# A hybrid RWKV-7 and MoBA layer on one Trainium2 core: the two heads of a pair take turns on the halves of TensorE's array

## The chip, the core and the metric

The kernel runs on one core of a Trainium2 chip. The core has a matrix engine (TensorE, PE in the profile), a vector engine (VectorE, DVE), an engine for functions of one variable (ScalarE, ACT), a general engine (GpSimd, POOL), SyncE (SP), which issues most transfers here, and 16 DMA engines. They work side by side, each takes its own instructions in their order, and semaphores make one wait for another. Matmuls write to PSUM, from which VectorE and ScalarE read; everything else lies in SBUF. Both have 128 partitions. The metric is device time in microseconds (us): 842.22 before, the median of 3 runs (840.99 to 842.25).

## What is computed

One decoder layer for 256 tokens of width 2048, in float32. One projection of the normalised input feeds two branches, whose results are gated, added and projected back:

```
h = rms_norm(x);  p = h @ w_in                         # 2048 x 12416
y_a = rwkv7_mix(p_r, p_k, p_v, p_wd, p_ad) * silu(z_a)  # 16 heads of 64
y_b = moba_attention(p_q, p_kq, p_vq) * silu(z_b)       # 16 heads of 64
merged = sigmoid(g_a) * (y_a @ w_proj_rwkv) + sigmoid(g_b) * (y_b @ w_proj_moba)
out = x + merged @ w_out
```

For 256 tokens the block-sparse attention has a single block, so it is causal attention with normalised queries and keys: softmax(q k / 8, masked) v for each head. The RWKV recurrence is computed in 4 chunks of 64 tokens: within a chunk the products of keys with keys and of keys with queries are needed, masked, and from these a triangular system is solved.

## The kernel before

**The dense work.** The weights stream through SBUF in loads of 1 MB. Each load makes two jobs. A job's half of the weights is split by ScalarE (`hi`, L216) and VectorE (`lo`, L222) into two parts, and TensorE multiplies in three passes, hi by hi, lo by hi and hi by lo: 24 matmuls of 128x256 (L329) where the result is wanted feature by feature, 12 of 128x512 (L347 to L349) where it is wanted token by token. Splits run two jobs ahead.

**The side work.** Everything else (RWKV, attention, norms) is written as generators (`rwkv_elem`, `rwkv_r`, `inverse`, `rwkv_v`, `moba`, ...). They stand in one queue, and after each job the next piece of the first of them, up to its `yield`, is written behind the job. Urgent ones (`trans` in `qk_post`, `group_norm`) advance after every job as well. The heads come in two groups of eight (g = 0, 1), and each piece of side work is done once for each group. The order that counts on the engines is not quite that of the code: a scheduler of the framework places instructions by its own estimates, and may put dense matmuls between those of a piece.

**Heads and halves.** Two heads of 64 features share 128 partitions: head p = 0 of a pair lies in partitions 0 to 63, p = 1 in 64 to 127; fi = 0 to 3 counts the pairs of a group. A matmul on one head's keys thus uses 64 rows of the array, and one that writes one head's values uses 64 columns. In the profile such shapes stand as rows*columns: 64*128, 128*64, 64*64; the dense matmuls are 128*128. A matmul on float32 leaves two records of PE in the trace, one on float32r (the dense ones) and a transpose one.

**What the change touches.** In `rwkv_r`, for each pair and head: four key products (L533, one for each chunk) into one PSUM bank of 128x512, which VectorE copies under a mask into `LL` (L536). In `moba`, a unit is one head half p of a group's four pairs, with u = 0: the first 128 queries against 128 keys, four heads (L825); u = 1 and 2: the last 128 queries against 256 keys, two heads each (L831). That makes six units a group. For a unit, VectorE copies the logits under the causal mask (L836) and takes the maximum (L838, L839), ScalarE takes the exponential and its sum (L843), VectorE divides (`normal`, L848, L849), TensorE transposes (`turn`, L858), ScalarE copies the transposed probabilities (L861, L864); and once the three units of a head half are done, `pv` multiplies them by the values (L874, L876), and ScalarE copies the result (L879). The loop at the end of `moba` interleaves the stages of units n, n-1 and n-2. Small products share four PSUM banks (`PSS`), the dense ones have four others (`PSM`).

`rwkv_v` (L670, L677, L694, L704) is not changed; there the two heads of a pair already follow each other instruction by instruction.

Of the kernel before, what the change touches and what calls it, by code (L numbers as in the profile page):

```python
# [36 lines left out]
def tile_hybrid_block(ctx: ExitStack, tc: tile.TileContext, x, pv, wdu, wau,  # L37
# [473 lines left out]
    def rwkv_r(g):  # L511
# [16 lines left out]
        for fi in range(4):  # L528
            for p in range(2):
                ps = PSS()  # L530
                sl = slice(64 * p, 64 * p + 64)
                for c in range(4):
                    pe.matmul(ps[:, c * P:(c + 1) * P],  # L533
                              bk[sl, fi, c].rearrange("p a t -> p (a t)"),
                              ar[sl, fi, c].rearrange("p a t -> p (a t)"), start=True, stop=True)
                dve.copy_predicated(  # L536
# [3 lines left out]
                    ps.rearrange("p (c t) -> p c t", c=4))  # L540
# [267 lines left out]
    def moba(g):  # L808
        q, k, v = M[g]["q"], M[g]["k"], M[g]["v"]
        s1 = T("cs", [P, 2, 2, S])  # L810
        smt = [T("sg", [P, 4, P]), s1[:, 0], s1[:, 1]]
        for ap in (smt[0], s1):
            pool.memset(ap, -1e30)
        yield
        us = [dict(p=p, u=u, nh=2 if u else 4, nk=S if u else P, sm=smt[u])
              for p in range(2) for u in range(3)]
        pts = {}
        prs = T("bk", [P, 4, 512])

        def logits(n, w):  # L820
            rows = slice(64 * w["p"], 64 * w["p"] + 64)
            ps = PSS()
            if w["u"] == 0:
                for fi in range(4):
                    pe.matmul(ps[:, fi * P:(fi + 1) * P], q[rows, fi, 0:P], k[rows, fi, 0:P],  # L825
                              start=True, stop=True)
                mask = mq[:, 1:2, :].to_broadcast([P, 4, P])
            else:
                for i in range(2):
                    fi = 2 * (w["u"] - 1) + i  # L830
                    pe.matmul(ps[:, i * S:(i + 1) * S], q[rows, fi, P:S], k[rows, fi, :],  # L831
                              start=True, stop=True)
                mask = mq.rearrange("p a t -> p (a t)").rearrange(
                    "p (o t) -> p o t", o=1).to_broadcast([P, 2, S])
            nh, nk, sm = w["nh"], w["nk"], w["sm"]
            dve.copy_predicated(sm, mask, ps.rearrange("p (f t) -> p f t", f=nh))  # L836
            mx = T("mx", [P, 4], bufs=2)
            dve.tensor_reduce(mx[:, 0:nh], sm, AX.X, ALU.max)  # L838
            dve.tensor_scalar(mx[:, 0:nh], mx[:, 0:nh], -0.125, None, ALU.mult)  # L839
# [12 lines left out]
        def turn(w):  # L852
            if w["u"] == 0:
                pts[w["p"]] = T("ar", [P, 4, 3, P])
# [27 lines left out]
        for n in range(9):  # L882
            if n in (5, 8):
                pv(0 if n == 5 else 1)
            if 2 <= n < 8:
                turn(us[n - 2])
# [206 lines left out]
```

## Time and profile before

| | us |
|---|---|
| median of 3 runs | 842.22 |
| the profiled execution | 843.0 |
| its span, first to last instruction | 841.3 |
| TensorE busy (matmuls) | 832.2 |
| VectorE busy | 554.3 |
| ScalarE busy | 422.2 |
| GpSimd busy | 29.0 |

The granted clock of TensorE was 1.000 over the whole span. A busy time counts every moment in which at least one instruction of the engine runs; a matmul's record lasts from its start to the modelled end of its passage through the array, so that records in a row overlap, and the interval between two starts is shorter than a record. The timeline merges equal instructions that follow each other into one row, with their number.

### The profile page before, as it was taken

The page shows a single profiled execution, that of the slowest core. Times are in us where ns is not written, and L with a number is a line of the kernel's source. Part 1 is how long each engine was busy: PE and PEld are TensorE (multiplying, and loading weights), DVE is VectorE, ACT ScalarE, POOL GpSimd, SP SyncE. Part 2 cuts the span into 40 slices and gives each one's busy share as a digit, 9 for nine tenths or more (in the row PEclk, how much of TensorE's full clock was granted, in tenths as well). Part 3 has the DMA queues.
Part 4 walks back from the last instruction along what each step waited for, and adds up shares of the span by engine and source line. Part 5 has one row for each costly group of instructions (what it writes and reads, how often), then busy time and mean ns, then how long its engine had stood idle before and what let it go on. Part 6 is the DMA issues. An engine that isn't in the chain of part 4 may idle for free.

```text
span 841.3 us, 15850 instructions
## 1 busy us (share of the span) xinstructions
PE 832.2 (99%) x6738; PEld 771.0 (92%) x6738; DVE 554.3 (66%) x776; ACT 422.2 (50%) x568; POOL 29.0 (3%) x42
## 2 busy tenths in 40 slices
PE   8999999999999999999999999999999999999998
PEld 7999878899998788899999988999999999998887
DVE  5869958956569569749974579554455566664553
ACT  6785435444437585435444477544444444443342
POOL 5001100000000002000000000000000000000000
PEclk9999999999999999999999999999999999999999
DMA  8564555564434344646564323555656655556772
GB/s 302 176 195 156 178 160 164 179 196 152 136 117 151 110 141 150 195 139 195 199 204 147 106 97 121 191 188 187 195 197 201 198 164 190 198 167 213 231 245 98
DMA packets 83206, 145.78 MB, mean 173 GB/s; under 512 B 11568, under 2 KB 13872, under 8 KB 83136
## 3 DMA queue, kind: packets, MB, share of 16 engines
q1 hardware_dynamic: 71584, 138.55, 50.7%
q10 hardware_dynamic: 11520, 6.16, 2.7%
q8 instruction: 53, 0.87, 0.4%
q14 instruction: 17, 0.14, 0.0%
q0 software_dynamic: 32, 0.05, 0.0%
HBM read 141.61 MB, written 3.15 MB: 172 GB/s over the span
## 4 chain that ended last, share of the span: by engine, by line
PE 98%; DVE 1%; DMA 1%; issue 0%; SPq 0%; ACT 0%
PE pm L329 59%; PE pm L348 9%; PE pm L347 9%; PE pm L349 9%; PE ps L533 2%; PE ps L670 1%; PE ps L831 1%; PE ps L874 1%; PE ps L677 1%; PE ps L858 1%; DMA raw<-in_w_in_dram 1%; PE ps L694 1%; PE ps L825 1%; PE ps L601 0%; PE ps L593 0%; PE ps L704 0%
## 5 line engine op out<-in xcount | busy, mean ns | idle before, releaser
L216 ACT ACTIVATE hi<-raw 128x1024 fp32r<-128x1024 f32 (+1 forms) x259 | 273.1, 1056 | 350.5 <-PE pm L329 214.7
L222 DVE TENSOR_TENSOR lo<-raw,hi 128x1024 fp32r<-128x1024 f32 (+1 forms) x259 | 314.5, 1217 | 203.1 <-ACT hi L216 199.5
L329 PE MATMUL pm<-xh,hi 128*128 128x256 f32 x1168 | 327.3, 282 | 1.0 <-ACT xh L144 1.0
L329 PE MATMUL pm<-xh,lo 128*128 128x256 f32 x1168 | 324.3, 279 | 1.0 <-DVE lo L222 1.0
L329 PE MATMUL pm<-xl,hi 128*128 128x256 f32 x1168 | 324.3, 279 | 0.0
L329 PEld LDWEIGHTS pm<-xh,hi 128*128 128x128 f32 x1168 | 219.7, 189 | 4.7 <-ACT xh L144 1.4
L329 PEld LDWEIGHTS pm<-xh,lo 128*128 128x128 f32 x1168 | 219.9, 189 | 2.6 <-DVE lo L222 1.4
L329 PEld LDWEIGHTS pm<-xl,hi 128*128 128x128 f32 x1168 | 219.8, 189 | 0.6
L348 PE MATMUL pm<-lo,xh 128*128 128x512 f32 x192 | 76.3, 398 | 0.0
L349 PE MATMUL pm<-hi,xl 128*128 128x512 f32 x192 | 75.6, 394 | 0.0
L347 PE MATMUL pm<-hi,xh 128*128 128x512 f32 x192 | 73.5, 398 | 0.0
L348 PE MATMUL pm<-lo,mgh 128*128 128x512 f32 (+1 forms) x128 | 48.4, 378 | 0.0
L349 PE MATMUL pm<-hi,mgl 128*128 128x512 f32 (+1 forms) x128 | 48.0, 376 | 0.0
L347 PE MATMUL pm<-hi,mgh 128*128 128x512 f32 (+1 forms) x128 | 44.4, 377 | 0.0
L348 PEld LDWEIGHTS pm<-lo,xh 128*128 128x128 f32 x192 | 36.1, 188 | 8.3 <-issue 0.5
L349 PEld LDWEIGHTS pm<-hi,xl 128*128 128x128 f32 x192 | 36.1, 188 | 7.5 <-issue 0.2
L347 PEld LDWEIGHTS pm<-hi,xh 128*128 128x128 f32 x192 | 35.9, 188 | 7.6 <-ACT ar L864 0.2
L347 PEld LDWEIGHTS pm<-hi,mgh 128*128 128x128 f32 x128 | 24.0, 188 | 4.7
L349 PEld LDWEIGHTS pm<-hi,mgl 128*128 128x128 f32 x128 | 24.0, 188 | 4.7
L348 PEld LDWEIGHTS pm<-lo,mgh 128*128 128x128 f32 x128 | 24.0, 188 | 4.4
L564 DVE TENSOR_TENSOR tmp<-sg,kk 64x31 f32<-64x31 f32 (+15 forms) x62 | 20.5, 331 | 5.9 <-DMA sg<-gd 4.7
L329 PE MATMUL pm<-bk,hi 128*128 128x256 f32 x128 | 22.8, 281 | 0.0
(280 smaller groups left out, 1014.3 us busy)
## 6 DMA issues: line engine op xcount, KB each, us to landing
raw<-in_w_in_dram SPq DMA_DIRECT2D x94, 1024.0 KB, 5.1
raw<-in_w_out_dram SPq DMA_DIRECT2D x16, 1024.0 KB, 5.3
raw<-in_w_proj_moba_dram SPq DMA_DIRECT2D x8, 1024.0 KB, 5.1
raw<-in_w_proj_rwkv_dram SPq DMA_DIRECT2D x8, 1024.0 KB, 5.0
raw<-in_w_in_dram SPq DMA_DIRECT2D x5, 512.0 KB, 6.6
k<-in_x_dram ACTq DMA_DIRECT2D x4, 256.0 KB, 4.2
r<-in_x_dram ACTq DMA_DIRECT2D x4, 256.0 KB, 3.8
k<-in_x_dram SPq DMA_DIRECT2D x2, 256.0 KB, 5.1
```

The lines of the kernel that those rows point to most:

```text
L216: act.activation(job["hi"][:, c], job["src"][:, c], AF.Copy)
L222: dve.tensor_tensor(job["lo"][:, c], job["src"][:, c], f32(job["hi"][:, c]), ALU.subtract)
L329: pe.matmul(o, (hi, hi, lo)[ps][:, i, cs], (mh, ml, mh)[ps](k), start=(k == 0 and fi % 2 == 0 and ps == 0), stop=(k == jb["last"] and ps = ...
L347: pe.matmul(o, sh[:, k, ts], hi[:, i, cs], start=(k == 0), stop=False)
L348: pe.matmul(o, sh[:, k, ts], lo[:, i, cs], start=False, stop=False)
L349: pe.matmul(o, sl[:, k, ts], hi[:, i, cs], start=False, stop=end)
L533: pe.matmul(ps[:, c * P:(c + 1) * P], bk[sl, fi, c].rearrange("p a t -> p (a t)"), ar[sl, fi, c].rearrange("p a t -> p (a t)"), start=True ...
L564: dve.tensor_tensor(tv, gcol.to_broadcast([64, nt, j + 1]), trow.to_broadcast([64, nt, j + 1]), ALU.mult)
L670: pe.matmul(ps[64 * p:64 * p + 64, c0 + 64 * fi:c0 + 64 * fi + 64], LL[p][:, fi, c, which, :], UV[:, c, p, fi, :], start=(fi == 0), stop=( ...
L677: pe.matmul(ps[sl, c0 + 64 * fi:c0 + 64 * fi + 64], ar[sl, fi, c, which, :], St[sl, fi, :], start=False, stop=True, skip_group_check=True)
L694: pe.matmul(ps[sl, cols], X64[sl, fi * 4 + c, :], Zs[sl, cols], start=True, stop=True)
L825: pe.matmul(ps[:, fi * P:(fi + 1) * P], q[rows, fi, 0:P], k[rows, fi, 0:P], start=True, stop=True)
```

## The change

In `rwkv_r` the loop over the two heads moves inside the loop over the chunks, with a PSUM bank for each head; the two copies by VectorE stand behind all eight matmuls. In `moba` a unit now holds both heads of each pair: three units a group, each with two banks of logits; the matmuls of logits and of probabilities times values alternate between p = 0 and p = 1. The values are multiplied unit by unit, each matmul with 128 columns to stream instead of 256 and 128, and both heads' results lie in one bank, which units 1 and 2 share. Logits, normalising, transposes of each head and values are written with a `yield` after each.

```diff
@@ -526,18 +526,20 @@
         r["rr"] = (rh, rl)
         yield
         for fi in range(4):
-            for p in range(2):
-                ps = PSS()
-                sl = slice(64 * p, 64 * p + 64)
-                for c in range(4):
-                    pe.matmul(ps[:, c * P:(c + 1) * P],
+
+            pss = [PSS() for _ in range(2)]
+            for c in range(4):
+                for p in range(2):
+                    sl = slice(64 * p, 64 * p + 64)
+                    pe.matmul(pss[p][:, c * P:(c + 1) * P],
                               bk[sl, fi, c].rearrange("p a t -> p (a t)"),
                               ar[sl, fi, c].rearrange("p a t -> p (a t)"), start=True, stop=True)
+            for p in range(2):
                 dve.copy_predicated(
                     LL[p][:, fi].rearrange("p c a t -> p c (a t)"),
                     m2.rearrange("p a t -> p (a t)").rearrange("p (o t) -> p o t", o=1)
                     .to_broadcast([P, 4, P]),
-                    ps.rearrange("p (c t) -> p c t", c=4))
@@ -807,87 +809,93 @@
 
     def moba(g):
         q, k, v = M[g]["q"], M[g]["k"], M[g]["v"]
-        s1 = T("cs", [P, 2, 2, S])
-        smt = [T("sg", [P, 4, P]), s1[:, 0], s1[:, 1]]
-        for ap in (smt[0], s1):
+
+
+
+        smt = [T(t, [P, 2, 512]) for t in ("sg", "cs")]
+        for ap in smt:
             pool.memset(ap, -1e30)
         yield
-        us = [dict(p=p, u=u, nh=2 if u else 4, nk=S if u else P, sm=smt[u])
-              for p in range(2) for u in range(3)]
-        pts = {}
-        prs = T("bk", [P, 4, 512])
-
-        def logits(n, w):
-            rows = slice(64 * w["p"], 64 * w["p"] + 64)
-            ps = PSS()
-            if w["u"] == 0:
-                for fi in range(4):
-                    pe.matmul(ps[:, fi * P:(fi + 1) * P], q[rows, fi, 0:P], k[rows, fi, 0:P],
-                              start=True, stop=True)
+        prs = T("bk", [P, 2, 2, 512])
+        pts = T("ar", [P, 2, 2, 4, P])
+        us = [dict(u=u, nh=2 if u else 4, nk=S if u else P) for u in range(3)]
+        halves = [slice(0, 64), slice(64, 128)]
+        po = []
+
+        def logits(w):
+            u, nh, nk = w["u"], w["nh"], w["nk"]
+            pss = [PSS() for _ in range(2)]
+            for i in range(nh):
+                fi = i if u == 0 else 2 * (u - 1) + i
+                for p, rows in enumerate(halves):
+                    pe.matmul(pss[p][:, i * nk:(i + 1) * nk],
+                              q[rows, fi, 0:P] if u == 0 else q[rows, fi, P:S],
+                              k[rows, fi, 0:nk], start=True, stop=True)
+            if u == 0:
                 mask = mq[:, 1:2, :].to_broadcast([P, 4, P])
             else:
-                for i in range(2):
-                    fi = 2 * (w["u"] - 1) + i
-                    pe.matmul(ps[:, i * S:(i + 1) * S], q[rows, fi, P:S], k[rows, fi, :],
-                              start=True, stop=True)
                 mask = mq.rearrange("p a t -> p (a t)").rearrange(
                     "p (o t) -> p o t", o=1).to_broadcast([P, 2, S])
-            nh, nk, sm = w["nh"], w["nk"], w["sm"]
-            dve.copy_predicated(sm, mask, ps.rearrange("p (f t) -> p f t", f=nh))
-            mx = T("mx", [P, 4], bufs=2)
-            dve.tensor_reduce(mx[:, 0:nh], sm, AX.X, ALU.max)
-            dve.tensor_scalar(mx[:, 0:nh], mx[:, 0:nh], -0.125, None, ALU.mult)
-            w["Pr"] = prs[:, n % 4, :].rearrange("p (a b) -> p a b", a=nh)
-            w["sum"] = T("smx", [P, 4], bufs=2)
-            for i in range(nh):
-                act.activation(w["Pr"][:, i, :], sm[:, i, :], AF.Exp, scale=0.125,
-                               bias=mx[:, i:i + 1], accum_out=w["sum"][:, i:i + 1])
-
-        def normal(w):
-            nh, nk = w["nh"], w["nk"]
-            dve.reciprocal(w["sum"][:, 0:nh], w["sum"][:, 0:nh])
-            dve.tensor_tensor(w["Pr"], w["Pr"], w["sum"][:, 0:nh].rearrange(
+            w["Pr"], w["sum"] = [], []
+            for p in range(2):
+                sm = smt[u > 0][:, p, :].rearrange("p (a b) -> p a b", a=nh)
+                dve.copy_predicated(sm, mask, pss[p].rearrange("p (f t) -> p f t", f=nh))
+                mx = T("mx", [P, 4], bufs=2)
...
+                Pr = prs[:, u % 2, p, :].rearrange("p (a b) -> p a b", a=nh)
+                sums = T("smx", [P, 4], bufs=4)
+                for i in range(nh):
+                    act.activation(Pr[:, i, :], sm[:, i, :], AF.Exp, scale=0.125,
+                                   bias=mx[:, i:i + 1], accum_out=sums[:, i:i + 1])
+                w["Pr"].append(Pr)
+                w["sum"].append(sums)
+
+        def normal(w, p):
+            nh, nk, sums, Pr = w["nh"], w["nk"], w["sum"][p], w["Pr"][p]
+            dve.reciprocal(sums[:, 0:nh], sums[:, 0:nh])
+            dve.tensor_tensor(Pr, Pr, sums[:, 0:nh].rearrange(
                 "p (h o) -> p h o", o=1).to_broadcast([P, nh, nk]), ALU.mult)
 
-        def turn(w):
-            if w["u"] == 0:
-                pts[w["p"]] = T("ar", [P, 4, 3, P])
-            pt = pts[w["p"]]
+        def turn(w, p):
             ps = PSS()
             for i in range(4):
                 pe.transpose(ps[:, i * P:(i + 1) * P],
-                             w["Pr"].rearrange("p a b -> p (a b)")[:, i * P:(i + 1) * P], ident)
-            if w["u"] == 0:
-                act.activation(pt[:, :, 0, :], ps.rearrange("p (f t) -> p f t", f=4), AF.Copy)
-            else:
-                f0 = 2 * (w["u"] - 1)
-                act.activation(pt[:, f0:f0 + 2, 1:3, :],
-                               ps.rearrange("p (f b t) -> p f b t", f=2, b=2), AF.Copy)
-
-        def pv(p):
-            rows = slice(64 * p, 64 * p + 64)
-            pt = pts[p]
-            po = [PSS() for _ in range(2)]
-            for fi in range(4):
-                o = po[fi // 2][rows, (fi % 2) * S:(fi % 2 + 1) * S]
-                col = slice(fi * P + 64 * p, fi * P + 64 * p + 64)
-                pe.matmul(o, v[:, 0, col], pt[:, fi, 0:2, :].rearrange("p a t -> p (a t)"),
-                          start=True, stop=True, skip_group_check=True)
-                pe.matmul(o[:, P:S], v[:, 1, col], pt[:, fi, 2, :], start=False, stop=True,
-                          skip_group_check=True)
-            for half in range(2):
-                act.activation(oT[rows, 4 * g + 2 * half:4 * g + 2 * half + 2, :].rearrange(
-                    "p f t -> p (f t)"), po[half][rows, :], AF.Copy)
-
-        for n in range(9):
-            if n in (5, 8):
-                pv(0 if n == 5 else 1)
-            if 2 <= n < 8:
-                turn(us[n - 2])
-            if 1 <= n < 7:
-                normal(us[n - 1])
-            if n < 6:
-                logits(n, us[n])
+                             prs[:, w["u"] % 2, p, i * P:(i + 1) * P], ident)
+            act.activation(pts[:, w["u"] % 2, p].rearrange("p a t -> p (a t)"), ps, AF.Copy)
+
+        def pv(w):
+            u = w["u"]
+            pt = pts[:, u % 2]
+            if u < 2:
+                po.append(PSS())
+            o = po[-1]
+            for i in range(4 if u == 0 else 2):
+                fi = i if u == 0 else 2 * (u - 1) + i
+                for b in range(1 if u == 0 else 2):
+                    for p, rows in enumerate(halves):
+                        col = slice(fi * P + 64 * p, fi * P + 64 * p + 64)
+                        pe.matmul(o[rows, fi * P:(fi + 1) * P], v[:, b, col],
+                                  pt[:, p, i if u == 0 else 2 * i + b, :],
+                                  start=(b == 0), stop=(b == (u > 0)), skip_group_check=True)
+            if u != 1:
+                t = slice(0, P) if u == 0 else slice(P, S)
+                act.activation(oT[:, 4 * g:4 * g + 4, t], o.rearrange("p (f t) -> p f t", f=4),
+                               AF.Copy)
+
+        logits(us[0])
+        yield
+        for n in range(3):
+            normal(us[n], 0)
+            normal(us[n], 1)
+            if n < 2:
+                logits(us[n + 1])
+            yield
+            turn(us[n], 0)
+            yield
+            turn(us[n], 1)
+            yield
+            pv(us[n])
             yield
 
 
```

The scheduler places the new instructions anew. Three places show what stands there now. The first is TensorE's order where the last key products of the second group are computed; `ps_3845` and `ps_3851` (before), `ps_3876` and `ps_3877` (now) are the banks of the two heads, the rows around them dense matmuls. Before:

```order
L329 MATMUL pm_3664<-xl,hi_3735 128x256
L329 MATMUL pm_3664<-xh,lo_3737 128x256
L533 MATMUL ps_3845<-ar_3522,bk_3594 128x128 x4
L533 MATMUL ps_3851<-ar_3522,bk_3594 128x128 x4
L329 MATMUL pm_3663<-xh,hi_3766 128x256
```

And now:

```order
L329 MATMUL pm_3663<-xh,lo_3768 128x256
L534 MATMUL ps_3876<-ar_3555,bk_3613 128x128
L534 MATMUL ps_3877<-ar_3555,bk_3613 128x128
L534 MATMUL ps_3876<-ar_3555,bk_3613 128x128
L534 MATMUL ps_3877<-ar_3555,bk_3613 128x128
L534 MATMUL ps_3876<-ar_3555,bk_3613 128x128
L534 MATMUL ps_3877<-ar_3555,bk_3613 128x128
L534 MATMUL ps_3876<-ar_3555,bk_3613 128x128
L534 MATMUL ps_3877<-ar_3555,bk_3613 128x128
L329 MATMUL pm_3662<-xh,hi_3808 128x256
```

The eight matmuls are the same, and they change heads after each instead of once. Five of the eight turns (two groups, four pairs) stand like this; the others are cut by dense matmuls into pieces of one to seven.

The second place is TensorE's order in the attention of the first group, where the logits of the last unit meet the first products with the values. Before (`ps_3037`: logits; `ps_3063`: values; L858: transposes):

```order
L858 MATMUL ps_3029<-ident,bk_2829 128x128 x4
L831 MATMUL ps_3037<-kn_1659,qn_1374 128x256 x2
L874 MATMUL ps_3063<-ar_2918,vq_1858 64x256
L876 MATMUL ps_3063<-ar_2918,vq_1858 64x128
L874 MATMUL ps_3063<-ar_2918,vq_1858 64x256
L876 MATMUL ps_3063<-ar_2918,vq_1858 64x128
L348 MATMUL pm_3015<-lo_3098,xh 128x512
```

Now (`ps_3057` and `ps_3058`: logits of the two heads; `ps_3027`: values; L863: transposes):

```order
L349 MATMUL pm_3014<-hi_3009,xl 128x512
L878 MATMUL ps_3027<-ar_2830,vq_1858 64x128
L831 MATMUL ps_3057<-kn_1659,qn_1374 128x256 x2
L831 MATMUL ps_3058<-kn_1659,qn_1374 128x256
L878 MATMUL ps_3027<-ar_2830,vq_1858 64x128 x7
L831 MATMUL ps_3058<-kn_1659,qn_1374 128x256
L863 MATMUL ps_3095<-ident,bk_2829 128x128 x4
```

The first of the eight products with values stands apart from the other seven, and here the logits of the next unit lie between and behind them. In all six units the eight are cut into one and seven; in four of them, dense matmuls alone lie between.

The third place is ScalarE's order in the attention of the second group, at its last unit. L843 and L849 are the exponentials, L907 and L915 the sigmoids of the gates, L216 the splits of weights, L940 and L948 copies for the last projections, the other rows copies out of PSUM. Before:

```order
L843 ACTIVATE bk_5418,smx_5632<-cs_5402,mx_5629 128x256 x2
L216 ACTIVATE hi_5734<-raw_5635 128x1024
L861 ACTIVATE ar_5677<-ps_5678 128x4x128
L940 ACTIVATE qn_5844<-oT 128x1024
L216 ACTIVATE hi_5768<-raw_5635 128x1024
L864 ACTIVATE ar_5677<-ps_5724 128x2x256
L843 ACTIVATE bk_5418,smx_5693<-cs_5402,mx_5690 128x256 x2
L216 ACTIVATE hi_5814<-raw_5732 128x1024
L907 ACT_TABLE_LOAD
L907 ACTIVATE LL_716_5406<-LL_716_5406 128x512 x2
```

Now, up to the last exponentials of the group:

```order
L915 ACTIVATE LL_713_5409<-LL_713_5409 128x512
L948 ACTIVATE qn_5966<-oT 128x1024
L865 ACTIVATE ar_5422<-ps_5710 128x512
L216 ACTIVATE hi_5795<-raw_5716 128x1024
L849 ACT_TABLE_LOAD
L849 ACTIVATE bk_5421,smx_5672<-cs_5406,mx_5669 128x256 x2
L865 ACTIVATE ar_5422<-ps_5746 128x512
L915 ACT_TABLE_LOAD
L915 ACTIVATE LL_713_5409<-LL_713_5409 128x512
L216 ACTIVATE hi_5829<-raw_5716 128x1024
L849 ACT_TABLE_LOAD
L849 ACTIVATE bk_5421,smx_5679<-cs_5406,mx_5676 128x256 x2
```

Sigmoids now stand between the exponentials of the last unit's two heads, and each switch from one function to the other loads a table; one more table load stands right ahead of the first of these rows. The program has 21 table loads instead of 17.

## Rows read from the trace of the kernel before

**Rows 1.** The page, part 1: busy us, share of the span, instructions.

```profile
PE 832.2 (99%) x6738; PEld 771.0 (92%) x6738; DVE 554.3 (66%) x776; ACT 422.2 (50%) x568; POOL 29.0 (3%) x42
```

**Rows 2.** The page, part 4: the chain that ended last, by engine.

```profile
PE 98%; DVE 1%; DMA 1%; issue 0%; SPq 0%; ACT 0%
```

**Rows 3.** Waits of TensorE: total us, times, longest.

```profile
PE ps L296 <- POOL ident masks.py:199: 2.8, 1, 2.8
PE pm L329 <- DVE lo L222: 1.0, 1, 1.0
...
```

**Rows 4.** Groups of TensorE's instructions: records | busy us, mean ns | idle before.

```profile
...
L533 PE MATMUL ps<-ar,bk 64*128 64x128 f32 x128 | 14.5, 288 | 0.0
...
L874 PE MATMUL ps<-ar,vq 128*64 128x256 f32 x32 | 9.9, 392 | 0.0
...
L831 PE MATMUL ps<-kn,qn 64*128 64x256 f32 x32 | 9.0, 402 | 0.0
...
L876 PE MATMUL ps<-ar,vq 128*64 128x128 f32 x32 | 6.1, 272 | 0.0
...
L825 PE MATMUL ps<-kn,qn 64*128 64x128 f32 x32 | 4.6, 285 | 0.0
...
```

**Rows 5.** Timeline of TensorE, L670 and L694: start, duration, engine, line, tiles, shapes, records.

```profile
197.63 0.69 PE L670 MATMUL ps<-UV,LL 128*64 128x64 f32 x16
...
201.54 0.28 PE L329 MATMUL pm<-xl,hi 128*128 128x256 f32 x1
...
202.00 0.28 PE L329 MATMUL pm<-xh,lo 128*128 128x256 f32 x1
202.20 0.68 PE L694 MATMUL ps<-Zs,X 64*64 64x64 f32 x16
202.81 0.38 PE L329 MATMUL pm<-xh,hi 128*128 128x256 f32 x1
203.03 0.29 PE L329 MATMUL pm<-xl,hi 128*128 128x256 f32 x1
```

**Rows 6.** L825: all records (min/median/max ns), one burst, its last six.

```profile
L825 PE MATMUL ps<-kn,qn x32: 272/272/373, 248.8 to 505.6; 64*128 64x128 f32 x32
...
248.81 1.16 PE L825 MATMUL ps<-kn,qn 64*128 64x128 f32 x8
...
249.03 0.83 PE L825 MATMUL ps<-kn,qn 64*128 64x128 f32 x6
```

**Rows 7.** Timeline of TensorE, one burst of L831.

```profile
252.83 1.13 PE L831 MATMUL ps<-kn,qn 64*128 64x256 f32 x4
```

**Rows 8.** Timeline of TensorE, one burst of L533, both heads.

```profile
357.35 1.71 PE L533 MATMUL ps<-ar,bk 64*128 64x128 f32 x16
```

**Rows 9.** Timeline of TensorE, one burst of L874 and L876: first and last row.

```profile
511.82 0.65 PE L874 MATMUL ps<-ar,vq 128*64 128x256 f32 x2
...
512.96 0.38 PE L876 MATMUL ps<-ar,vq 128*64 128x128 f32 x2
```

**Rows 10.** Timeline of ScalarE, attention of the second group.

```profile
491.49 1.15 ACT L907 ACTIVATE LL<-LL 128x512 f32<-128x512 f32 x2
...
498.51 1.28 ACT L843 ACT_TABLE_LOAD   x1
...
504.20 0.51 ACT L843 ACTIVATE bk<-cs,mx 128x256 f32<-128x256 f32 x1 [2.35 <-DVE mx L839]
...
505.11 0.19 ACT L843 ACTIVATION_READ_ACCUMULATOR bk<-cs,mx 128x1 f32 x1
505.21 1.04 ACT L216 ACTIVATE hi<-raw 128x1024 fp32r<-128x1024 f32 x1
506.15 0.57 ACT L864 ACTIVATE ar<-ps 128x512 f32<-128x512 f32 x1
...
509.56 1.06 ACT L940 ACTIVATE BK<-yaT 128x1024 fp32r<-128x1024 f32 x1 [0.24 <-DVE yaT L939]
```

**Rows 11.** Timeline of VectorE, same stretch: a unit is divided.

```profile
505.53 0.69 DVE L849 TENSOR_TENSOR bk<-bk,smx 128x512 f32<-128x512 f32 x1
```

More of the change, by code (lines that the diff above doesn't have):

```diff
@@ L539, in rwkv_r @@
                     .to_broadcast([P, 4, P]),
-                    ps.rearrange("p (c t) -> p c t", c=4))
+                    pss[p].rearrange("p (c t) -> p c t", c=4))
             yield
@@ L846, in normal @@
-        def normal(w):
-            nh, nk = w["nh"], w["nk"]
-            dve.reciprocal(w["sum"][:, 0:nh], w["sum"][:, 0:nh])
-            dve.tensor_tensor(w["Pr"], w["Pr"], w["sum"][:, 0:nh].rearrange(
+            w["Pr"], w["sum"] = [], []
[3 more added lines that the diff above has]
+                mx = T("mx", [P, 4], bufs=2)
+                dve.tensor_reduce(mx[:, 0:nh], sm, AX.X, ALU.max)
+                dve.tensor_scalar(mx[:, 0:nh], mx[:, 0:nh], -0.125, None, ALU.mult)
+                Pr = prs[:, u % 2, p, :].rearrange("p (a b) -> p a b", a=nh)
[5 more added lines that the diff above has]
+                w["sum"].append(sums)
```

## The prediction

> **What bounds the kernel now.** I read the busy times first. TensorE is busy for 832.2 of 841.3 us, VectorE and ScalarE for 66% and 50% [rows 1]. A busy TensorE alone proves little, so the chain of waits comes next: 98% of it is TensorE [rows 2], and the list of what TensorE waited for holds four entries, all in the first microseconds, of which the two longest stand here [rows 3]. From then on TensorE never waits for anybody, so this kernel's time is the time of its instruction stream, one interval after the other. What the change saves or adds on TensorE therefore shows in full, and what it does on other engines shows only where TensorE is made to wait.
>
> Next comes the work that the change touches. The listing of TensorE's groups gives it: L533 (RWKV key products), L825 and L831 (logits), L874 and L876 (probabilities times values) [rows 4]. Each float32 matmul leaves two records there, so 64 instructions of L533 are 128 records. These stand in the stream as bursts between the dense 128*128 matmuls of the projections, and the timeline gives the price of a burst. Take a burst of L694: four dense intervals lie between 201.54 and 202.00, 0.115 each; the last dense matmul ahead starts at 202.00, the first one behind at 202.81 and the next at 203.03. So the burst costs 0.81 - 0.115, plus 0.105 by which the first dense interval behind it is longer: 0.80, while its records are busy for 0.68 [rows 5]. A burst's price is its busy time + 0.12.
>
> L825 shows what one half of the array does: eight records busy for 1.16, the last six of them for 0.83, one alone for 0.272 [rows 6]. So a record of 128 columns takes a slot of (0.83 - 0.27)/5 = 0.112, and the burst's price of 1.28 is 8 x 0.112 plus a fixed 0.38 for going into the 64-row shape and back. L831's four records of 256 columns are busy for 1.13 [rows 7]: (1.25 - 0.38)/4 = 0.2175 a slot. L694 and L670 alternate between halves already: 16 records are busy for 0.68 and 0.69 [rows 5]. At 64 columns a slot is some 0.056 (half of 0.112, an estimate); sixteen in a row would need 0.9, eight pairs need 0.45, and with the fixed part only the pairs fit: 0.80 = 8 x 0.056 + 0.35. So two halves do run side by side at full rate, both in the 64*64 shape and in the 128*64 shape. For the 64*128 shape, L533 says the same: 16 records, two groups of instructions on different halves, one behind the other, are busy for 1.71 [rows 8], not 1.16 + 8 x 0.112 = 2.06. About three records of the second half ran beside the first half's.
>
> **The change, part by part.** First what it takes away. By busy time + 0.12 a burst: L533, 11 bursts, 14.5 + 1.3 = 15.8. L825, 4 bursts, 4.6 + 0.5 = 5.1. L831, 8 bursts, 9.0 + 1.0 = 10.0 [rows 4]. L874 with L876: one burst runs from 511.82 to 512.96 + 0.38, 1.52 busy, 1.64 with the rest [rows 9]; 8 such are 13.1. Two bursts stand directly beside other small-tile work and share a change of shape, 0.3 less. Sum 43.7 us.
>
> Then what stands there instead. A burst now costs its fixed part and the slots of its busier half, and how the scheduler cut the bursts decides much. Key products: 12 bursts; five hold a full turn of eight instructions and a sixth seven, 8 slots each, the other six are pieces of one to four instructions, four with 4 slots and two with 2: 68 slots, 12 x 0.38 + 68 x 0.112 = 12.2. Logits of 128 keys: 2 bursts of 1.28 = 2.6. Logits of 256 keys: two clean groups of 4 slots, and two that it tore apart between values' products, 6 and 8 slots: 22 x 0.2175 = 4.8. Values' products: each of the six groups is cut into one instruction alone and seven later, 2 + 8 slots: 60 x 0.112 = 6.7. Fixed parts of these last two kinds: one logits burst alone 0.38, eight bursts of values' products alone 8 x 0.35 = 2.8, three bursts that mix both shapes with 5 + 3 + 3 changes of shape at some 0.18 (half of a fixed part) = 2.0, and 0.05 net for two logits bursts of the second group that stand directly behind rwkv_v's products. Sum 31.5. The difference is 12.2 us: 3.6 from the key products and 8.6 from the attention. Alternation alone in whole bursts would be worth more; the pieces with one instruction alone eat some 3 us of it (six times a fixed part of 0.35 and two slots).
>
> At one place a rule of the Trainium skill stands against this sum. The values' products of the two heads differ in columns of the array, not in rows; L670 is of that shape, and its 16 records take 0.69, no longer than eight pairs of L694 [rows 5]. "TensorE: Matmul & The Clock Gate", section The mechanism, says that weights are loaded beside a running matmul only where the row groups differ, and that matmuls are never reordered. By that rule the values' products would need 96 slots instead of 60, 4.0 us more, and the saving would be 8.2; by the row it is 12.2, and I go by the row.
>
> Now the other engines. VectorE has the same copies, maxima and divisions; ScalarE has 4 copies of results instead of 8 and the same exponentials. Both have slack while TensorE does the next projection job, and their work hides there. But ScalarE loads its tables 21 times instead of 17, since the exponentials of the second group now stand between the gates' sigmoids. The last of them decides: ps_5893's transposes on TensorE wait for VectorE's division, that for two exponentials, and those have in front of them on ScalarE, from the copy of the first values' product on: four table loads of 1.28, two sigmoids of 0.6 (1.15 for two), two pairs of exponentials of 1.1 (504.20 to 505.30), three copies of 1.06 and two of 0.6, 12.9 in all, some 0.8 less because each starts 0.1 before the one ahead ends (505.21 + 1.04 against 506.15) [rows 10]; then 0.7 and a reciprocal of about 0.2 on VectorE [rows 11]. With the 0.9 in which the last value product ends and its bank is copied, that is 13.9. TensorE has in the same stretch 75 dense matmuls (8.6), 12 transposes (1.3), a logits piece (1.2) and two bursts of values' products (0.6 and 1.25): 12.9. So TensorE waits 1.0 us there. Behind it in TensorE's queue stands the projection itself, so that microsecond is paid in full. The trace of before has no such wait: I bound it by 0 (if VectorE's and ScalarE's orders fit better than I sum) and by 3 (three units with such a wait each), and take 1.0, since it comes from rows of the same instructions.
>
> PSUM: a unit now takes two banks of four at once, and a values' bank is held over two units. A bank is emptied by one copy, and the next unit's logits stand a job or more of dense work later, so I cost this at nothing; if that cover goes, it is part of the 3 us above.
>
> The profiled execution took 843.0 (841.3 span and 1.7 around it): 843.0 - 12.2 + 1.0 = 831.8. The median of before is 842.2, 0.8 under it, so I predict 831.0.
>
> **The rivals.** (1) Pairs overlap but not at full rate, say with slots a quarter longer. The 68 + 16 + 60 slots of 0.112 and 22 of 0.2175, 20.9 us, then cost 5.2 more, the wait shrinks to nothing, and the gain is 7.0: 835.2. The same page of the Trainium skill, section Measured speedup vs the span model, gives 2.38 for three column tiles, 0.79 a tile; by that figure it would be 5.6 instead of 5.2. Against the rival stand the eight pairs of L694 and L670 in 0.68; for it, that both halves at 128 and 256 columns at once are shown only for three records of L533.
> (2) The column halves, which take their input from the same rows, do not pair: 96 slots instead of 60, a gain of 8.2, no wait, 834.0. Only L670 speaks against it, at 64 columns. (This is what the skill's rule above would make of it.)
> (3) More waits. TensorE works through the same units with less time between them, and its in-order queue meets exponentials that stand behind table loads at three or four places instead of one: 4 to 5 us of waiting, 834 to 835. For it: ScalarE's queue in that stretch is full, by the sum above.
> (4) Slower: the halves are served one after the other, because an instruction's two records block the other half's. Then the key products need 128 slots, the logits 32 and 32, the values' products 96: 60 x 0.112 + 16 x 0.112 + 10 x 0.2175 + 36 x 0.112 = 14.7 us more than I sum; also the overlap of before at each change of half is gone with that. 843.0 + 2.5 = 845.5, or 844.7 by the median. It decides once fewer than about a sixth of the pairs overlap. L694, with the same two records an instruction, speaks against it.
> (5) The row halves gain nothing because they write two banks, the column halves do: 10.7 lost of the 12.2, no change, 840.7 or so.
>
> **Chances.** My forecast, 829 to 833.5: 0.70. Rival 1: 0.08. Rival 2: 0.05. Rival 3: 0.10. Rival 4: 0.04. Rival 5: 0.03. The range runs from 828.8 (no wait at all, and half a microsecond more from bursts that join) to 836.2, which takes in rivals 1 to 3. No change means within 0.2% (1.7 us), about what a measurement of this kernel can tell. Faster by more 0.92, same 0.04, slower 0.04.
>
> **What would show it.** Right: bursts of the key products with 16 records busy for 1.16 instead of 1.71; four-instruction logits bursts busy for 1.13 with eight records; values' bursts of seven instructions busy for some 1.16; TensorE's list of waits with one new entry of about 1 us, by VectorE, near the second group's last unit; dense intervals unchanged. Wrong: 16 alternating records in over 1.4 us (rivals 4 and 5 for the key products, 2 for the values' products); several new waits of TensorE for ScalarE or VectorE adding to over 3 us (rival 3); or dense matmuls that wait for hi or lo because their splits come late behind the extra table loads.

## The result, and the profile after

The changed kernel takes 834.58 us (median of four executions, 834.21 to 836.63), the kernel before 841.61 beside it on the same chip: ratio 0.9924, interval 0.9902 to 0.9945. It is faster by 7.0 us, where 11.2 were forecast. The forecast's 831.0 is 3.6 us short; its range holds the time. The profiled execution, the slowest of the four, took 836.63 (span 834.9), 6.4 less than the one of before.

The busy line and the chain that ended last (the page, parts 1 and 4) answer to [rows 1, 2]:

```profile
PE 821.7 (98%) x6770; PEld 763.3 (91%) x6770; DVE 550.3 (66%) x776; ACT 423.4 (51%) x568; POOL 28.9 (3%) x42
...
PE 92%; ACT 3%; DVE 2%; DMA 2%; issue 1%; SPq 0%; ACTq 0%; DVEq 0%
```

TensorE's busy time fell by 10.5 us, the span by 6.4. The rest is in the chain: before, 98% of it was TensorE; now 7% goes through ScalarE, VectorE and transfers. TensorE waits, and the list of its waits (total us, times, longest), against [rows 3], says where:

```profile
PE ps L296 <- POOL ident masks.py:199: 2.8, 1, 2.8
PE ps L595 <- DMA cs<-td: 2.2, 1, 2.2
PE ps L863 <- ACT hi L216: 1.6, 1, 1.6
PE pm L329 <- DVE lo L222: 1.0, 1, 1.0
PE ps L750 <- DVE a L743: 0.5, 1, 0.5
PE ps L878 <- ACT ar L865: 0.5, 1, 0.5
PE pm L329 <- ACT xh L144: 0.4, 1, 0.4
```

The entries at L296 and L329 were there before. New are four: one at the merge (L595 is the first product of `merge`, L593 before) and three around the second group's attention, 4.8 us in all.

The changed groups of TensorE (records | busy us, mean ns | idle before), against [rows 4] (L534 is the key products, L831 the logits, L878 the values' products):

```profile
L534 PE MATMUL ps<-ar,bk 64*128 64x128 f32 x128 | 10.8, 290 | 0.0
...
L878 PE MATMUL ps<-ar,vq 128*64 128x128 f32 x96 | 9.1, 282 | 0.5 <-ACT ar L865 0.5
...
L831 PE MATMUL ps<-kn,qn 64*128 64x256 f32 x32 | 6.3, 405 | 0.0
...
L831 PE MATMUL ps<-kn,qn 64*128 64x128 f32 x32 | 2.3, 285 | 0.0
```

Summed over the groups, 28.5 us busy instead of 44.1. Single bursts in TensorE's timeline, against [rows 6 to 9]:

```profile
361.67 1.16 PE L534 MATMUL ps<-ar,bk 64*128 64x128 f32 x16
...
485.97 1.16 PE L831 MATMUL ps<-kn,qn 64*128 64x128 f32 x16
...
530.96 1.09 PE L878 MATMUL ps<-ar,vq 128*64 128x128 f32 x14
```

Sixteen records on two row halves take 1.16, as long as eight on one half did [rows 6], and 14 on two column halves take 1.09. Pairs run side by side at full rate in both shapes.

Now the merge. TensorE's timeline there, then its windows (us, busy and records of each engine, granted clock, DMA share, GB/s):

```profile
437.11 1.19 PE L595 MATMUL ps<-cs,LL 32*32 32x32 f32 x32 [2.21 <-DMA cs<-td]
...
439.06 0.42 PE L329 MATMUL pm<-xh,hi 128*128 128x256 f32 x1
439.27 0.41 PE L329 MATMUL pm<-xl,hi 128*128 128x256 f32 x1
```

```profile
436.00:438.00 2.00, 0.89 (x28) 0.89 (x29) 0.91 (x2) 0.14 (x1) 0.00 (x0) 1.00 0.66 101
438.00:440.00 2.00, 2.00 (x19) 1.96 (x16) 2.00 (x2) 0.59 (x1) 0.00 (x0) 0.63 0.00 0
440.00:442.00 2.00, 2.00 (x12) 2.00 (x11) 1.91 (x4) 0.00 (x0) 0.00 (x0) 0.52 0.40 55
442.00:444.00 2.00, 2.00 (x33) 1.87 (x32) 1.97 (x4) 1.06 (x1) 0.00 (x0) 1.00 1.00 386
```

TensorE stood still for 2.2 us, and behind that the granted clock is 0.63 and 0.52, which is the lower of its two levels (1.2 GHz) for most of both windows: dense matmuls start 0.21 apart instead of 0.115. It lasts 3.4 us and costs half of that, 1.7. So this place costs 3.9 us.

What it waited for shows in the transfers of 420 to 445 us (issues, KB each, median us to landing), of the kernel before and then of the changed one:

```profile
td<-kk ACTq DMA_DIRECT2D x1, 256.0 KB, 2.9
cs<-td ACTq DMA_DIRECT2D x4, 64.0 KB, 3.9
```

```profile
td<-kk ACTq DMA_DIRECT2D x1, 256.0 KB, 5.4
cs<-td ACTq DMA_DIRECT2D x4, 64.0 KB, 5.1
```

The inverse goes through memory: a store to td, four loads back into Dn, which is all that `merge` waits for. Before, the store was issued at 432.38, 3.9 us after a 1 MB weight load (428.43). In the changed kernel it is issued at 426.34, 0.6 us after one (425.72). Store and loads together now take 3.7 us longer (the sum of the two medians).

The records of the DMA packets show why (queue, packets, MB, share of 16 engines; q1 carries the weight loads, q10 what ScalarE issues). The first window of the changed kernel, 426 to 430 us, has no row for q10; the second, 430.5 to 432 us, has:

```profile
q1 hardware_dynamic: 436, 0.89, 75.9%
```

```profile
q10 hardware_dynamic: 63, 0.19, 31.7%
```

The store's data moved only when nearly all of the weight load ahead of it had.

The merge's first product needs the first of the four loads. In the changed kernel that landed at 437.07 and the product started at 437.11. Before, that load was issued at 435.31 and landed after 4.1, at 439.4, 1.2 us ahead of the product:

```profile
440.65 2.11 PE L593 MATMUL ps<-cs,LL 32*32 32x32 f32 x64
```

So the merge has not come closer to the store. From the store's issue to the first product it was 8.3 us before (432.38 to 440.65), and it would be 8.6 now (426.34 to 434.9, where TensorE stopped). What the store and the first load need grew from 7.0 to 10.7.

### The profile page after: what moved, and what is told of

Same layout as the page of the kernel before. It is cut to its first block, busy times and chain, and to the rows that moved or that the text cites. A ratio compares the mean times of both kernels' runs of the same rounds, so it can differ in the third digit from the quotient of the medians.

```text
span 834.9 us, 15904 instructions
## 1 busy us (share of the span) xinstructions
PE 821.7 (98%) x6770; PEld 763.3 (91%) x6770; DVE 550.3 (66%) x776; ACT 423.4 (51%) x568; POOL 28.9 (3%) x42
## 4 chain that ended last, share of the span: by engine, by line
PE 92%; ACT 3%; DVE 2%; DMA 2%; issue 1%; SPq 0%; ACTq 0%; DVEq 0%
PE pm L329 56%; PE pm L348 9%; PE pm L347 9%; PE pm L349 9%; PE ps L534 1%; PE ps L672 1%; PE ps L679 1%; ACT bk L849 1%; PE ps L878 1%; DMA td<-kk 1%; DMA cs<-td 1%; PE ps L831 1%; PE ps L696 1%; DVE lo L222 1%; ACT hi L216 1%
## 5 line engine op out<-in xcount | busy, mean ns | idle before, releaser
L216 ACT ACTIVATE hi<-raw 128x1024 fp32r<-128x1024 f32 (+1 forms) x259 | 272.6, 1055 | 339.1 <-PE pm L329 193.1
L329 PE MATMUL pm<-xh,hi 128*128 128x256 f32 x1168 | 326.8, 282 | 0.4 <-ACT xh L144 0.4
L329 PE MATMUL pm<-xl,hi 128*128 128x256 f32 x1168 | 324.9, 280 | 0.0
L329 PE MATMUL pm<-xh,lo 128*128 128x256 f32 x1168 | 323.9, 280 | 1.0 <-DVE lo L222 1.0
L329 PEld LDWEIGHTS pm<-xh,hi 128*128 128x128 f32 x1168 | 220.4, 190 | 3.2 <-issue 0.8
L329 PEld LDWEIGHTS pm<-xh,lo 128*128 128x128 f32 x1168 | 220.0, 190 | 2.6 <-DVE lo L222 1.4
L329 PEld LDWEIGHTS pm<-xl,hi 128*128 128x128 f32 x1168 | 220.8, 190 | 1.0 <-issue 0.3
L329 PE MATMUL pm<-bk,hi 128*128 128x256 f32 x128 | 22.8, 281 | 0.0
```

The lines of the kernel that those rows point to most:

```text
L216: act.activation(job["hi"][:, c], job["src"][:, c], AF.Copy)
L329: pe.matmul(o, (hi, hi, lo)[ps][:, i, cs], (mh, ml, mh)[ps](k), start=(k == 0 and fi % 2 == 0 and ps == 0), stop=(k == jb["last"] and ps = ...
```

## The experiments

Two theories at the start. A: pairs run at full rate and the stream saved its 12 us, but new waits (and the half clock behind them) eat some 6 of it. B: pairs run below full rate. The ratios are to the kernel before, run beside each set.

**e1_products: the key products alone.** The kernel before with this edit:

```
-            for p in range(2):
-                ps = PSS()
...
+            pss = [PSS() for _ in range(2)]
+            for c in range(4):
+                for p in range(2):
```

> Only the key products of rwkv_r alternate; the attention is that of before. Theory A (the shorter TensorE stream shows in full, and what was lost went into new waits of TensorE: 2.2 us for the transfers td and cs ahead of the second group's merge plus 1.7 us of half clock behind that wait, and 2.4 us inside the second group's attention): bursts of L533's kind 12.4 instead of 15.9 us, no new wait in the attention, so 3.5 us faster than before if the merge does not wait, and no more than 0 to 1 us faster if it waits as in the changed kernel. Theory B (pairs on two halves give less than the records show, the stream itself is short by 5 us): 1.5 us faster or less with no new wait.

840.81 us, ratio 0.9989 (0.9974 to 1.0004): no difference. Its list of waits, and one window behind the longest of them:

```profile
PE pm L329 <- DVE lo L222: 3.2, 2, 2.3
```

```profile
384.00:386.00 2.00, 2.00 (x12) 2.00 (x10) 2.00 (x6) 0.80 (x1) 0.00 (x0) 0.50 0.00 0
```

The merge did not wait; another transfer did the same damage. VectorE stood at the inverse's first step, which needs G back from memory (5.6 us from issue to landing, with a weight load issued 0.06 us behind it; in the kernel before 3.4 us, with the load 1.2 us behind), and the `lo` of a projection job was queued behind that step. TensorE lost 2.3 us and 1.7 by the half clock, 4.0: all of the 3.6 that the edit was forecast to save. This execution (843.15) is among the three slowest of twelve (838.47 to 843.36), so its stop need not stand in all of them.

**e2_attention: the attention alone.** The changed kernel with the loop above put back as it was.

> Only the attention is changed; the key products stand as before. Theory A: stream 8.8 us shorter, some 2.4 us of waits in the second group's attention stay, so 6.4 us faster than before if the merge of the second group does not wait for td and cs, 2.5 us faster if it does with the half clock behind it. Theory B: 4 us faster, with no wait at the merge.

840.02 us, ratio 0.9985 (0.9970 to 0.9999). Of its waits:

```profile
PE ps L594 <- DMA cs<-td: 2.4, 2, 2.0
PE ps L862 <- ACT hi L216: 1.6, 1, 1.6
```

Both groups' merges wait (0.4 and 2.0), each with a half-clock stretch behind it, and the attention's waits are all there. The parts alone give 1.1 and 1.9 us on medians, both together 7.0. The parts don't add up: what each moves decides which transfer falls beside which load. In e1 the store of the second group is issued 3.9 us behind a load, as before, and the merge does not wait; in e2 it is issued 0.6 behind one.

**e3_merge10: the merge later.** `for _ in range(5): yield` between the inverse's loads and the merge became `range(10)`.

> The changed kernel, but the merge of a group is written 10 jobs instead of 5 behind the inverse, so that its first matmul comes some 2.6 us later in TensorE's stream. Theory A: the wait of L595 goes (below 0.3 us) and with it the stretch at half clock; 3 to 4 us faster than the changed kernel, 830.5 to 831.5; waits in the second group's attention stay or move. Theory B or a half clock that has other reasons: no change, 834.6, or the clock falls in another place.

834.11 us, ratio 0.9917 (0.9895 to 0.9939): the same as the change. The waits:

```profile
PE pm L329 <- DVE lo L222: 3.9, 5, 1.3
...
PE ps L595 <- DMA cs<-td: 1.2, 1, 1.2
```

The wait moved more than it shrank, from 2.2 to 2.5 at the second group's merge (1.2 for cs, 1.3 for `lo`). The scheduler put the merge only one job later (23 dense matmuls), and VectorE's transposes of Dn, still waiting, hold the `lo` splits behind them. Half clock again.

**v2_together_m10: that, and one step fewer in each attention unit.** As e3_merge10, without the `yield` between the two calls of `turn`, so that both halves are transposed in one step.

> As e3, and both heads of a unit are transposed in one step, without a yield between, so that a unit's values' products are not held apart and moba needs three steps less a group, which takes the second group's last exponentials out from between the gates' sigmoids. Theory A: besides e3's gain the 2 to 2.4 us of waits in the attention go, and bursts with one instruction alone get fewer: 827.5 to 829. Theory B: as the changed kernel to within 1 us, 833.5 to 834.6.

836.02 us, ratio 0.9929 (0.9911 to 0.9948). None of the three attention waits is left, yet it is no faster:

```profile
PE pm L329 <- DVE lo L222: 2.7, 3, 1.3
PE ps L595 <- DMA cs<-td: 1.8, 1, 1.8
```

So B is not needed and A is incomplete: moving the merge does not take its wait away. The next four kernels take away what is waited for; they do not compute the layer.

**x1_after_td and x2_after_both: without the ways through memory.** In x1 a small copy stands in for store and loads; x2 leaves out the way of G as well.

```
-        act.dma_start(td.rearrange("b h t s -> (b h) t s"), Ti)
...
+        pool.memset(Dn, 0.0)
+        pool.tensor_copy(Dn[0:64, 0, :], Ti[:, 31, :])
```

> The changed kernel with the inverse's way through memory left out (the store to td and the four loads into Dn): a small GpSimd copy of the inverse's last row into a zeroed Dn stands in, so the merge still waits for the inverse's last step, but not for transfers; what the merge computes is therefore not the reference's. Theory S (the merge waited for the two transfers behind a weight load, and the half-clock stretch behind that wait is its consequence): no TensorE wait over 0.5 us at pbt's matmuls, granted clock 1.0 at 438 to 442 us, and 3.9 us less than the changed kernel, some 830.5. Rival D (the inverse's own last step on VectorE is late, the transfers are beside the point): the wait stays at 1 us or more and the time at 834. Rival C (the half clock comes whatever TensorE waits for): the wait goes, the half-clock stretch stays, some 832.4.

> As the run before, and the way of the triangular factors through gd into G left out as well (a small GpSimd copy of the last factor's last rows into a zeroed G stands in; the solve runs on other numbers, at the same length). Theory S: no wait of VectorE at the inverse's first step, no wait of TensorE for lo behind it, no half-clock stretch inside the RWKV part; what is left over the bare stream is the attention's waits (1.6, 0.5 and 0.5 us): 829.5 to 831. Rival D: 834.

x1: 828.14 us, ratio 0.9836 (0.9821 to 0.9850). x2: 828.28, 0.9839 (0.9824 to 0.9854). All waits of x1 that are listed, and the window behind its merge, which starts at 430.83:

```profile
PE ps L296 <- POOL ident masks.py:199: 2.7, 1, 2.7
PE pm L329 <- ACT xh L144: 1.4, 1, 1.4
PE pm L329 <- DVE lo L222: 1.0, 1, 1.0
PE pm L329 <- DVE xl L149: 0.8, 1, 0.8
```

```profile
432.00:434.00 2.00, 2.00 (x40) 1.96 (x37) 0.82 (x1) 1.18 (x2) 0.00 (x0) 1.00 0.98 381
```

No wait is left behind the first 90 us, and the half clock is gone (mean granted clock 1.000): theory S holds, D and C fall. The expected time was missed on the low side by 2.4 us, about the attention's waits (2.6), and those went as well. The reason stands in ScalarE's groups. The changed kernel loads its tables 21 times, x1 and x2 19 times; the scheduler placed anew, and two sigmoids stand under one table load. So x1 alone changed two things: how the 6.4 us that it gains divide between merge and attention is read from the profile of the changed kernel, not from times. The clean comparison is x2 with its control.

**x3_before_both: the control,** the kernel before with both ways left out in the same manner.

> The control: the kernel before, with both ways through memory left out in the same manner. Theory S: before, these trips were just covered, so it gains next to nothing: 840.5 to 842. If it gains 3 us or more too, the transfers cost both kernels alike and can't be what ate the change's gain.

840.63 us, ratio 0.9988 (0.9978 to 0.9997): next to nothing, as expected. Between x3 and x2 lies the change with no wait over 0.2 us in either kernel behind the first 90 us: 840.63 - 828.28 = 12.35 us.

**x4_both_together: x2 with both transposes in one step.**

> The changed kernel without both ways through memory (as above), and with the transposes of both halves of an attention unit in one step instead of two, which takes a step out of each unit and so changes where ScalarE's chain stands against TensorE. Theory S and the bare stream: no wait over 0.5 us is left outside the start; against the control it shows the whole stream gain, 12 us less (829 to 830 if the control is 841.5). A rival, that two-row-half pairs below full rate cost some of the gain: 8 to 10 us less than the control with no wait to be seen.

825.35 us, ratio 0.9801 (0.9787 to 0.9816), 15.3 under the control where 12 were expected. No wait over 0.2 us is left here behind the first 90 us, as in x2, so the 2.9 us beyond x2 come from the stream. Priced as in the prediction (busy time + 0.12 a burst), its attention bursts cost 17.7 us and those of x2 19.2: in each group one lone values' instruction now stands with its other seven. The other 1.4 us are not broken down. The rival of slow pairs is out.

**v1_together, y2_split, y3_together_split: nothing left out.** The first is the change with both transposes in one step. The second issues each 1 MB weight load as two of 512 KB. The third does both.

```
-        cuts = ... else (0, 2, 4) if j < 3 else (0, nk)
+        cuts = ... else (0, 2, 4) if j < 3 else (0, nk // 2, nk)
```

> The changed kernel with the transposes of both halves of an attention unit in one step instead of two; nothing is left out. In the pair of runs without the ways through memory that edit took 2.9 us off (828.3 to 825.4). If bursts cost by their number (four transposes twice, or eight at once), the same 2 to 3 us come off here: 831 to 832.5. If the merge's wait for the transfers grows as the stream before it gets shorter, it eats that gain as well: 834, with 3 us or more of waits at the merge and behind it. The attention's waits (1.6, 0.5 and 0.5 us) go by either.

> The changed kernel with every 1 MB weight load issued as two of 512 KB, nothing left out: the store to td then stands behind half a load at a time, if the DMA engines take turns between the queues at all. Theory S with turns: the store moves within 2 us of its issue instead of 4 to 5, the merge's wait and the half-clock stretch go, and the time falls to 830 to 831.5. Theory S without turns (a transfer stands behind all that was issued before it, however cut): the store moves as late as before, the wait stays at 2 us, and the time at 834 to 835.

> Both edits of the two runs before together, nothing left out: the version meant to be faster than either kernel. With turns between the queues 827.5 to 829; without, the same as the kernel with the transposes in one step alone, 831 to 834.

v1: 834.09 us, ratio 0.9904 (0.9881 to 0.9927), spread over 829.72 to 837.02. y2: 831.63, 0.9882 (0.9864 to 0.9900). y3: 830.20, 0.9861 (0.9846 to 0.9877), the lowest median of those that compute everything, 11.7 us under the kernel before. In v1 the merge's wait is as long as ever, with no half clock behind it in the profiled execution (829.72, its fastest):

```profile
PE ps L595 <- DMA cs<-td: 2.3, 1, 2.3
```

```profile
436.00:438.00 2.00, 2.00 (x36) 1.96 (x34) 2.00 (x3) 0.59 (x1) 0.00 (x0) 1.00 0.00 0
```

In its five other executions the mean granted clock is 0.997 or 0.998 and the time 831.7 to 837.0. In their code v1 and x4 differ by the ways through memory alone, and their gains over the kernel before lie 8.1 us apart (7.8 and 15.9). The wait in this profile is 2.3 of that; what the slower executions lose no profile shows. In y2, the merge's wait and the store's time:

```profile
PE ps L595 <- DMA cs<-td: 1.1, 1, 1.1
```

```profile
td<-kk ACTq DMA_DIRECT2D x1, 256.0 KB, 4.6
```

In y3 they are 2.0 and 5.4. The store does not move within 2 us of its issue, so what was expected from "turns between the queues" did not come. The expected gain came all the same (831.63, where 830 to 831.5 were expected), in part for another reason: y2 loads ScalarE's tables 19 times and has 0.2 us of attention waits. Why y3 is 3.9 us faster than v1 on medians, with much the same wait in its profile, is not settled.

## Why the prediction was right or wrong

**The stream: right.** Forecast -12.2, measured -12.35 (x3 against x2). That is no luck of terms that cancel: summed over TensorE's timelines, busy time + 0.12 a burst, the key products cost 15.8 before and 12.2 in the changed kernel (forecast 15.8 and 12.2), the attention's bursts 28.0 and 19.2 (forecast 27.9 and 19.3), and in x2 both cost what they do in the changed kernel. The burst of 16 key products was forecast busy for 1.16 and is 1.16; a values' burst of seven instructions 1.16, measured 1.09. Rivals 1, 2, 4 and 5 are out. Two column halves do pair: one after the other, 14 records would need 14 x 0.112, 1.57, and a fixed part, and the burst is busy for 1.09. The rule quoted from the Trainium skill ("TensorE: Matmul & The Clock Gate", section The mechanism) says that weights load beside a running matmul only where row groups differ. For the column halves it does not hold here, and choosing [rows 5] over it was right.

**The wait behind ScalarE: right in place, short in size.** Forecast 1.0 at the transposes of the second group's last unit. It came there, at L863, with 1.6, and two of 0.5 beside it (L750, L878). The list names "ACT hi" as the releaser; ScalarE's timeline shows the chain that was summed:

```profile
513.07 1.28 ACT L915 ACT_TABLE_LOAD   x1
...
517.39 1.28 ACT L849 ACT_TABLE_LOAD   x1
...
520.28 1.28 ACT L915 ACT_TABLE_LOAD   x1
...
523.17 1.28 ACT L849 ACT_TABLE_LOAD   x1
...
525.37 0.19 ACT L849 ACTIVATION_READ_ACCUMULATOR bk<-cs,mx 128x1 f32 x1
```

Four table loads, then the last exponentials end at 525.56, then VectorE's division, and TensorE goes on at 526.63. The stretch that was summed begins with the end of this burst, at 511.58:

```profile
510.49 1.09 PE L878 MATMUL ps<-ar,vq 128*64 128x128 f32 x14
```

```profile
511.51 1.06 ACT L948 ACTIVATE BK<-yaT 128x1024 fp32r<-128x1024 f32 x1 [3.89 <-DVE yaT L947]
512.47 0.58 ACT L883 ACTIVATE oT<-ps 128x512 f32<-128x512 f32 x1
```

To 526.63 it is 15.05, forecast 13.9. TensorE's own work in it is the forecast 12.9, so the waits in it are 2.1 (0.5 at L878, 1.6 at L863) instead of 1.0. Of the 1.1 that the sum was short, 0.6 is the bank's copy (L883), which stood behind another copy (L948). All three waits, 2.6 us, lie inside the bounds of 0 to 3.

**The step that failed: "one new TensorE wait".** The prediction went through the engines beside the bursts, VectorE, ScalarE and PSUM, and put the rest at nothing. It left out the transfers that `inverse` and `rwkv_r` send through memory, which the diff does not touch, but whose place among the weight loads moves with everything ahead of them. The merge's wait was worth 2.2 and the half clock behind it 1.7. Summed for the profiled executions: -12.35 + 3.9 + 2.6 = -5.9, measured -6.4; the half microsecond left is not accounted for. Rival 3 named the time (834 to 835, more waits), but placed all of them at exponentials; more than half were at the merge. The range holds the time, but the narrower 829 to 833.5, which had the chance of 0.70, does not.

The mistake in reading was to take a stream without waits for one with room. [Rows 3] say that TensorE did not wait, not by how much, and the margin at the merge was 1.2 us. What the same transfers take beside a load also stood in the trace of before, in its first group (transfers of 168 to 192 us), where the store is issued 0.9 us behind one:

```profile
td<-kk ACTq DMA_DIRECT2D x1, 256.0 KB, 5.2
cs<-td ACTq DMA_DIRECT2D x4, 64.0 KB, 5.0
```

From the store's issue to the first load's landing it took 10.6 there (176.75 to 187.33). Such a way against the second group's room of 8.3 makes a wait of 2.3; measured were 2.2. That the store would fall so close behind a load was not forecast.

Two smaller slips changed nothing. Of the four entries in [rows 3] one, the 1.0 at L329, stands at 89 us and not in the first microseconds, in both kernels. And the lower end of the range, 828.8, is not what its reason gives: without the wait and with half a microsecond more the sum is 829.5.

**PSUM at nothing: right.** No wait of TensorE is put down to a bank.

## What to carry to other kernels

When a stream bound by one engine gets shorter, list each point where that engine, or an in-order engine that feeds it, takes data from a transfer, and write its margin beside it: landing against first use. The change moves transfers against each other, even far from the edit. So count the margin against what such a transfer takes beside a large one (here 3.7 us more, against a margin of 1.2), and not only against what it took in the trace; a list of waits does not show it. To learn what a change is worth by itself, leave the suspected transfers out of both kernels and compare those two.

## What the runs showed of the hardware

- A store of 256 KB issued 0.6 us behind a 1 MB load took 5.4 us to land, one issued 3.9 us behind it 2.9. The kernels that keep this store have 18 of them: the 14 issued 0.2 to 1.2 us behind a load took 4.6 to 5.5, the four issued 2.6 to 3.9 behind one took 2.9. Cutting the load into two of 512 KB changed little in the second group (4.6 in y2, 5.4 in y3).
- A stop of TensorE of 2.2 us was followed by 3.4 us at the lower clock in the changed kernel, one of 2.3 us by none in v1, and one of 0.4 us, between the two halves of the first group's merge, again by 3.4 us in e2. So the length of the stop alone does not decide it in these runs.
- The profiled execution of x4 took 829.77 where the other five took 825.0 to 825.8. From about 520 to 645 us its dense matmuls came more slowly with a granted clock of 1.00; here x2 and then x4, 540 to 560 us:

```profile
540.00:560.00 20.00, 20.00 (x179) 20.00 (x179) 9.92 (x11) 9.26 (x10) 0.00 (x0) 1.00 0.66 210
```

```profile
540.00:560.00 20.00, 20.00 (x172) 20.00 (x171) 9.88 (x9) 8.46 (x9) 0.00 (x0) 1.00 0.57 192
```

  172 records instead of 179 in 20 us; 4% over that stretch is about the difference. What does that is open.
